# Softmax scaling moved to ScalarE, rotations with one addition, and other slots for the queued stages in a two-layer decoder trunk

## The chip, the cores and the metric

One core of one Trainium2 chip runs the whole program in one launch. The metric is the device time of that launch in microseconds; less is better. The kernel before took 453.48 us, the median of 3 runs.

## What is computed

The reference is a trunk of two layers over 256 positions and 1024 channels, all in float32. Layer 0 projects the input once and feeds two groups of heads: 4 heads of RetNet retention (with a pairwise rotation of queries and keys, a normalisation per head and a SiLU gate) and 8 heads of latent attention (low-rank queries and keys, a rotary part of 64 channels, causal softmax, SiLU gate). Layer 1 is an attention of 16 heads with 64 channels, whose queries and keys are rotated; with 256 positions its block selection comes down to causal softmax over the own block. Each layer ends in a LayerNorm of the scaled input plus the layer's output.

```python
def rope(x, pos):
    ang = pos[:, None, :, None] * inv
    cos, sin = jnp.cos(ang), jnp.sin(ang)
    x1, x2 = x[..., : d // 2], x[..., d // 2:]
    return jnp.concatenate([x1 * cos - x2 * sin, x1 * sin + x2 * cos], -1)
...
s = jnp.where(kpos[None, :] <= qpos[:, None], s, NEG)
p = jax.nn.softmax(s, axis=-1)
return jnp.einsum('bhqk,bhkd->bhqd', p, v)
```

## The kernel before, in words

**Products.** Every product of float32 matrices is three TensorE products: each operand is split into a high part (ScalarE's Copy into a rounded type, L165) and a low part (the rest, by VectorE, L166), and `mm3` (L158 to L162) adds high by high, low by high and high by low into the same PSUM tile. This split is made of every weight tile (names w_h and w_l, from the loaded tile raw) and of every intermediate that is multiplied again.

**Weights.** They come over SyncE's queue in units of mostly 128x1024 numbers, in the order of a list made ahead. A unit is split into one of 6 buffers (WBUFS), so ScalarE's copy of a unit into w_h can start only when TensorE has finished the unit six before it. In the odd layer a unit is 24 products of 256 columns.

**Order of the work.** TensorE's order is the order of the program text. VectorE's and ScalarE's orders come from a scheduler, which places their instructions by its own estimate; each engine then runs its list strictly in order. Work that hangs on earlier results is not written where it arises but handed to a list with `add(task, wait)`: `tick()`, which is called after each unit's products, runs the next piece of the oldest task that is due, and at most one piece that asks for a wait. The constants in L35 to L38 are these waits, counted in ticks: SCO, QR, VAL, LAT1, LAT2, MRG, MPT in the even layer, CROT, CSC, CPT and CAV in the odd one.

**The odd layer.** It runs in 4 quarters q of 4 heads, each of 8 units: two for each of the queries, keys, values (tiles pj) and the gate (pg). `rotated` (L821) applies `rope` (L313) to the projected queries or keys: two multiplications (into crot and rope_b) and two additions of halves into crot (L326). `later` then transposes crot on TensorE (tile pt, 4 transpositions) and splits it to cq_h, cq_l or ck_h, ck_l. `attend_odd` (L781) has three pieces, each for two pairs of heads: `first` writes the scores (tiles sc, 24 small products) and calls `softmax` (L516); `second` transposes the probabilities (`prob_T`, tiles ppt, 12 transpositions, split to pT_h, pT_l); `third` multiplies them with the values (poc), gates (cog, with cgate) and splits the result (oT). CPT[q] ticks stand between the first piece and the second, CAV between the second and the third. PSUM tiles of the tag "at" (sc, ppt, pt, poc and more) share 4 buffers.

**Softmax.** For each pair of heads VectorE takes the masked, negated scores and their minimum (L528), ScalarE the exponential with its sum (L531), VectorE doubles and inverts the sums (L534, L535) and multiplies the probabilities by the inverse (L538): 2 heads x 2 blocks of rows, of 128 and 256 columns, in place. There are 4 such calls in the even layer and 8 in the odd one, so 24 heads and 48 instructions of L538.

**Rotation tables.** At the program's start `angles` (L276) reduces the angles twice, once for 128x64 and once for 128x256 numbers, with 9 VectorE instructions each, and the negated sine is a further VectorE instruction (L306, L311). In the even layer `retention` (L432) rotates its queries and keys with two additions of halves (L451), and `merge` (L487) multiplies the normalised heads (ro) with their gate and transposes them.

Of the kernel before, what the change touches and what calls it, by code (L numbers as in the profile page):

```python
# [9 lines left out]
F32 = mybir.dt.float32  # L10
# [3 lines left out]
AF = mybir.ActivationFunctionType  # L14
OP = mybir.AluOpType
AX = mybir.AxisListType

P = 128
S = 256
NT = S // P  # L20
# [9 lines left out]
MAGIC = 12582912.0  # L30
PI_HI = 3.1415925
WBUFS = 6
TAIL = 5
HOLD = 5
SCO = 7, 4, 4, 5  # L35
CPT = 2, 2, 2, 4
MRG = 1, 1, 1, 5
LAT1, LAT2, QR, VAL, MSC, MPT, MAV, CROT, CSC, CAV = 3, 4, 8, 2, 1, 3, 1, 1, 1, 2  # L38
WARM = 9

OFF = np.cumsum([0, 1024, 1024, 2048, 2048, 256, 256, 64, 1024])
# [102 lines left out]
def trunk(ctx, tc, x, lng, lnb, w, cst, dec, out):  # L144
    nc = tc.nc
# [3 lines left out]
    wk = even.enter_context(tc.tile_pool(name="even", bufs=1))  # L149
# [76 lines left out]
    halfpi = cp.tile([P, 1], F32, name="halfpi")  # L226
# [21 lines left out]
    def cc(name):  # L248
        a, b = CST[name]
        return cs[:, a:b]  # L250
# [4 lines left out]
    posn_i, pos_i = cc("posn").bitcast(I32), cc("pos").bitcast(I32)  # L255
# [6 lines left out]
    for i, (raw, n, ks, cols) in enumerate(first):  # L262
        k = ks[0]
# [7 lines left out]
        for i2 in range(len(cols) // 288):  # L271
            j = max(i2, int(i == 1))
            for t in range(NT):
                mm3(pm[t][j][:, :288], x_rows(k), wv, lambda z: z[:, t * P:(t + 1) * P],
                    lambda z: z[:, i2 * 288:(i2 + 1) * 288], start=k == 0, stop=k == KD - 1)
    def angles(dst_cos, dst_sin, ang, shape):  # L276

        k = wk.tile(shape, F32, name="ang_k", tag="neg", bufs=4)
        nc.vector.tensor_scalar(k, ang, 1.0 / (2 * math.pi), MAGIC, op0=OP.mult, op1=OP.add)
        nc.vector.tensor_scalar(k, k, -MAGIC, None, op0=OP.add)  # L280
        rest = 2 * math.pi
        parts = []
        for bits in (2.0 ** -2, 2.0 ** -5, 2.0 ** -15, 2.0 ** -22):
            c = math.floor(rest / bits) * bits
            parts.append(c)
            rest -= c
        parts.append(rest)
        for c in parts:
            nc.vector.scalar_tensor_tensor(ang, k, -c, ang, op0=OP.mult, op1=OP.add)
        nc.vector.tensor_scalar(ang, ang, -PI_HI, PI_HI, op0=OP.max, op1=OP.min)  # L290
        nc.vector.scalar_tensor_tensor(k, ang, -1.0, ang, op0=OP.mult, op1=OP.max)
        nc.scalar.activation(dst_sin, ang, AF.Sin)
        nc.scalar.activation(dst_cos, k, AF.Sin, bias=halfpi, scale=-1.0)

    H2 = MR // 2
    cosr = wk.tile([P, S], F32, name="cosr")
    sinr = wk.tile([P, 2, S], F32, name="sinr")
    cosn = cp.tile([P, NT, H2], F32, name="cosn")
    sinn = cp.tile([P, NT, 2, H2], F32, name="sinn")
    posn = cp.tile([P, NT], F32, name="posn")  # L300
    nc.vector.tensor_copy(posn, posn_i)
    angn = wk.tile([P, NT, H2], F32, name="angn", tag="neg", bufs=4)
    for t in range(NT):
        nc.vector.tensor_scalar(angn[:, t, :], cc("inv"), posn[:, t:t + 1], None, op0=OP.mult)
    angles(cosn, sinn[:, :, 0, :], angn, [P, NT, H2])
    nc.vector.tensor_scalar(sinn[:, :, 1, :], sinn[:, :, 0, :], -1.0, None, op0=OP.mult)  # L306
    ang = wk.tile([P, S], F32, name="ang", tag="neg", bufs=4)
    nc.vector.tensor_copy(ang, pos_i)
    nc.vector.tensor_scalar(ang, ang, cc("inv_r"), None, op0=OP.mult)
    angles(cosr, sinr[:, 0, :], ang, [P, S])  # L310
    nc.vector.tensor_scalar(sinr[:, 1, :], sinr[:, 0, :], -1.0, None, op0=OP.mult)  # L311

    def rope(src, t, nt, nh, dst, tag=None):  # L313

        b = wk.tile([P, nt * nh * MR], F32, name="rope_b", tag=tag or f"rope_b{nt * nh}")

        def v(z, d):
            return z.rearrange("p (t n d) -> p t n d", t=nt, d=d)

        c4 = cosn[:, t:t + nt, None, :].to_broadcast([P, nt, 2 * nh, H2])  # L320
        nc.vector.tensor_tensor(v(dst, H2), v(src, H2), c4, op=OP.mult)
        s4 = sinn[:, t:t + nt, :, :].rearrange("p t a d -> p t (a d)")[:, :, None, :].to_broadcast([P, nt, nh, MR])
        nc.vector.tensor_tensor(v(b, MR), v(src, MR), s4, op=OP.mult)
        bv, dv = [z.rearrange("p (n a d) -> p n a d", a=2, d=H2) for z in (b, dst)]
        for i in range(2):
            nc.vector.tensor_tensor(dv[:, :, i, :], dv[:, :, i, :], bv[:, :, 1 - i, :], op=OP.add)  # L326

    def transposed(srcs, n, hi, lo):

# [102 lines left out]
    def retention(h, mid=None):  # L432
# [12 lines left out]
        for n, p in enumerate(v4):  # L445
            a = wk.tile([P, 2, S], F32, name="rot_a", tag="rot_a")
            b = wk.tile([P, 2, S], F32, name="rot_b", tag="rot_b")
            nc.vector.tensor_tensor(a, p, cosr[:, None, :].to_broadcast([P, 2, S]), op=OP.mult)
            nc.vector.tensor_tensor(b, p, sinr, op=OP.mult)
            for i in range(2):  # L450
                nc.vector.tensor_tensor(a[:, i, :], a[:, i, :], b[:, 1 - i, :], op=OP.add)  # L451
            qkT.append([z[:, 2 * n:2 * n + 2, :] for z in both])
            split_to(*qkT[n], a)
        qT, kT = qkT
# [61 lines left out]
    def softmax(sc, scale, tag, pb):  # L516
# [18 lines left out]
        nc.vector.reciprocal(rinv, sm)  # L535
        for j in range(nh):
            for i, (a, b) in enumerate(parts):
                nc.vector.tensor_scalar(prob[:, j, a:b], prob[:, j, a:b], rinv[:, i, j:j + 1], None, op0=OP.mult)  # L538
        return prob

    def causal_scores(o, q, k):
# [384 lines left out]
```

## Time and profile before

| | before |
|---|---|
| runs | 453.01, 453.48 and 2466.26 us; median 453.48 |
| the profiled execution | 453.44 us |
| its span (first to last instruction) | 451.7 us |
| granted TensorE clock, mean over the span | 0.994 |
| TensorE busy | 440.0 us |
| VectorE busy | 342.9 us |
| ScalarE busy | 230.0 us |

The 1.74 us between the profiled execution and its span lie outside of the instructions. Times in the rows below are counted from the span's start. Matmuls are pipelined, so one of them shows as longer than the distance to the next one; a wait of TensorE is therefore read from the distance of two starts, compared with the same distance elsewhere.

### The profile page before, as it was taken

Reading aid. Unit: us, or ns where it says so; the run is one execution under the profiler, and the core shown is the slowest. Engines: PE = TensorE matmul, PEld = TensorE weight load, DVE = VectorE, ACT = ScalarE, POOL = GpSimd, SP = SyncE. Lnnn points to the kernel's source line nnn. Section 1 sums busy time; section 2 is a strip of 40 time slices with the busy share of each in tenths; the row PEclk is TensorE's granted clock in tenths of the full one; section 3 lists DMA queues with packets and bytes.
Section 4 is the critical chain, followed back from the end, with each engine's and each line's share of the span. In section 5 each row is a group of like instructions: output and inputs, shape, how many; then the busy total and the mean of one; then the engine's idle time right before and its main releaser. Section 6 shows DMA issues by size and latency. Waiting matters only on the chain.

```text
span 451.7 us, 7705 instructions
## 1 busy us (share of the span) xinstructions
PE 440.0 (97%) x2987; PEld 397.3 (88%) x2987; DVE 342.9 (76%) x663; ACT 230.0 (51%) x386; POOL 10.0 (2%) x18
## 2 busy tenths in 40 slices
PE   8999999999999999999999999999998999999993
PEld 6997889988998888889998888889998999999883
DVE  4899698885878765566697687577997797897847
ACT  5677456553654543435465566214572564744610
POOL 0010000000000000000000000000000000000001
PEclk9999999999999999999999999999998999999999
DMA  8986634544555565555556568705834435354002
GB/s 288 362 226 227 232 131 158 179 121 136 147 181 150 177 229 174 179 186 152 156 156 227 167 202 256 248 1 148 275 123 111 157 125 172 107 187 141 1 0 94
DMA packets 21780, 75.55 MB, mean 167 GB/s; under 512 B 2416, under 2 KB 2800, under 8 KB 21744
## 3 DMA queue, kind: packets, MB, share of 16 engines
q1 hardware_dynamic: 20304, 70.66, 48.7%
q10 hardware_dynamic: 1440, 4.41, 2.9%
q8 instruction: 23, 0.38, 0.3%
q14 instruction: 13, 0.11, 0.1%
HBM read 74.01 MB, written 1.05 MB: 166 GB/s over the span
## 4 chain that ended last, share of the span: by engine, by line
PE 92%; DVE 5%; DMA 1%; ACT 1%; issue 1%; POOL 0%; SPq 0%; DVEq 0%
PE pg L160 5%; PE pg L162 5%; PE pg L161 5%; PE pj L160 5%; PE pj L161 5%; PE pj L162 5%; PE acc L160 4%; PE acc L161 4%; PE acc L162 4%; PE pv L160 3%; PE pv L162 3%; PE pv L161 3%; PE pa L161 2%; PE pa L162 2%; PE pa L160 2%; PE sc L552 2%
## 5 line engine op out<-in xcount | busy, mean ns | idle before, releaser
L166 DVE TENSOR_TENSOR w_l<-raw,w_h 128x1024 fp32r<-128x1024 f32 (+3 forms) x134 | 156.2, 1168 | 59.9 <-ACT w_h L165 59.4
L165 ACT ACTIVATE w_h<-raw 128x1024 fp32r<-128x1024 f32 (+3 forms) x134 | 135.6, 1016 | 115.3 <-issue 32.0
L160 PE MATMUL pj<-w_h,xT_hi 128*128 128x256 f32 x192 | 55.2, 288 | 0.0
L161 PE MATMUL pj<-w_h,xT_lo 128*128 128x256 f32 x192 | 54.0, 281 | 0.0
L162 PE MATMUL pj<-w_l,xT_hi 128*128 128x256 f32 x192 | 53.9, 281 | 0.0
L160 PEld LDWEIGHTS pj<-w_h,xT_hi 128*128 128x128 f32 x192 | 36.7, 191 | 0.2
L161 PEld LDWEIGHTS pj<-w_h,xT_lo 128*128 128x128 f32 x192 | 36.7, 191 | 0.1
L162 PEld LDWEIGHTS pj<-w_l,xT_hi 128*128 128x128 f32 x192 | 36.8, 191 | 0.0
L160 PE MATMUL pv<-w_h,xT_hi 128*128 128x512 f32 x64 | 26.0, 406 | 0.0
L160 PE MATMUL pg<-w_h,xT_hi 128*128 128x512 f32 x64 | 25.8, 403 | 0.0
L162 PE MATMUL pv<-w_l,xT_hi 128*128 128x512 f32 x64 | 25.3, 395 | 0.0
L161 PE MATMUL pv<-w_h,xT_lo 128*128 128x512 f32 x64 | 25.3, 395 | 0.0
L161 PE MATMUL pg<-w_h,xT_lo 128*128 128x512 f32 x64 | 25.3, 395 | 0.0
L162 PE MATMUL pg<-w_l,xT_hi 128*128 128x512 f32 x64 | 25.3, 395 | 0.0
L160 PE MATMUL pg<-xT_hi,w_h 128*128 128x256 f32 x64 | 18.3, 287 | 0.0
L160 PE MATMUL pq<-xT_hi,w_h 128*128 128x256 f32 x64 | 18.2, 284 | 0.0
L160 PE MATMUL pmg<-xT_hi,w_h 128*128 128x256 f32 x64 | 18.1, 283 | 0.0
L161 PE MATMUL pq<-xT_hi,w_l 128*128 128x256 f32 x64 | 17.9, 280 | 0.0
L160 PE MATMUL pkk<-xT_hi,w_h 128*128 128x256 f32 x64 | 17.9, 280 | 0.0
L161 PE MATMUL pkk<-xT_hi,w_l 128*128 128x256 f32 x64 | 17.9, 280 | 0.0
L162 PE MATMUL pmg<-xT_lo,w_h 128*128 128x256 f32 x64 | 17.9, 279 | 0.0
L161 PE MATMUL pmg<-xT_hi,w_l 128*128 128x256 f32 x64 | 17.9, 279 | 0.0
(298 smaller groups left out, 1187.5 us busy)
## 6 DMA issues: line engine op xcount, KB each, us to landing
raw<-w SPq DMA_DIRECT2D x125, 512.0 KB, 3.6
raw<-w SPq DMA_DIRECT2D x7, 416.0 KB, 6.5
raw<-w SPq DMA_DIRECT2D x4, 256.0 KB, 2.7
xn<-x ACTq DMA_DIRECT2D x2, 512.0 KB, 4.3
decay<-dec ACTq DMA_DIRECT2D x1, 512.0 KB, 7.4
decay_ln<-lng ACTq DMA_DIRECT2D x1, 512.0 KB, 6.4
rv_h_ln<-lnb ACTq DMA_DIRECT2D x1, 512.0 KB, 3.9
lng_ln<-lng ACTq DMA_DIRECT2D x1, 512.0 KB, 4.6
```

Source lines behind the costliest of these rows:

```text
L160: nc.tensor.matmul(o, ca(a[0]), cb(b[0]), start=start, stop=False, skip_group_check=True)
L161: nc.tensor.matmul(o, ca(a[1]), cb(b[0]), start=False, stop=False, skip_group_check=True)
L162: state["mm"] = nc.tensor.matmul(o, ca(a[0]), cb(b[1]), start=False, stop=stop, skip_group_check=True)
L165: done = nc.scalar.activation(hi, src, AF.Copy)
L166: nc.vector.tensor_tensor(lo, src, hi.bitcast(F32), op=OP.subtract)
L552: nc.tensor.matmul(o[a][:, c:c + n], q[x][rs, t * P:(t + 1) * P], k[y][rs, :n], start=start and t == 0 and i == 0, stop=i == 2, skip_group ...
```

## The change

It has four parts.

1. `softmax`: the 48 multiplications of the probabilities by the inverse sum go from VectorE (L538) to ScalarE, as a Copy with a scale per row.
2. `rope` and `retention`: the two additions of halves become one addition over the whole tile, which reads the second operand with its halves in reverse. That is 18 additions instead of 36 for the tiles of 128x512, and 2 instead of 4 for the narrow ones of the latent keys.
3. The angles of both rotations lie in one tile of 128x320, reduced once; the negated sines come from ScalarE's Sin with scale -1 instead of from VectorE.
4. The slots: in the odd layer CPT is 3, 4, 4, 4 instead of 2, 2, 2, 4. In the even layer SCO is 6, 4, 4, 6 instead of 7, 4, 4, 5; MRG ends in 6 instead of 5; LAT1 is 5 instead of 3, LAT2 3 instead of 4, QR 10 instead of 8, VAL 3 instead of 2, MPT 2 instead of 3, MAV 2 instead of 1.

```diff
-SCO = 7, 4, 4, 5
-CPT = 2, 2, 2, 4
-MRG = 1, 1, 1, 5
-LAT1, LAT2, QR, VAL, MSC, MPT, MAV, CROT, CSC, CAV = 3, 4, 8, 2, 1, 3, 1, 1, 1, 2
+SCO = 6, 4, 4, 6
+CPT = 3, 4, 4, 4
+MRG = 1, 1, 1, 6
+LAT1, LAT2, QR, VAL, MSC, MPT, MAV, CROT, CSC, CAV = 5, 3, 10, 3, 1, 2, 2, 1, 1, 2
...
+    na = S + NT * H2
+    ang = wk.tile([P, 2 * S], F32, name="ang", tag="rot_a")[:, :na]
+    rounds = wk.tile([P, 2 * S], F32, name="rounds", tag="rot_b")[:, :na]
...
+    for cos, sin, z, za in ((cosn, [sinn[:, :, i, :] for i in range(2)], angn, absn),
+                            (cosr, [sinr[:, i, :] for i in range(2)], ang[:, :S], rounds[:, :S])):
+        for i, d in enumerate(sin):
+            nc.scalar.activation(d, z, AF.Sin, scale=(1.0, -1.0)[i])
+        nc.scalar.activation(cos, za, AF.Sin, bias=halfpi, scale=-1.0)
...
-        for i in range(2):
-            nc.vector.tensor_tensor(dv[:, :, i, :], dv[:, :, i, :], bv[:, :, 1 - i, :], op=OP.add)
+        nc.vector.tensor_tensor(dv, dv, bv[:, :, ::-1, :], op=OP.add)
...
-            for i in range(2):
-                nc.vector.tensor_tensor(a[:, i, :], a[:, i, :], b[:, 1 - i, :], op=OP.add)
+            nc.vector.tensor_tensor(a, a, b[:, ::-1, :], op=OP.add)
...
-                nc.vector.tensor_scalar(prob[:, j, a:b], prob[:, j, a:b], rinv[:, i, j:j + 1], None, op0=OP.mult)
+                nc.scalar.activation(prob[:, j, a:b], prob[:, j, a:b], AF.Copy, scale=rinv[:, i, j:j + 1])
```

On TensorE no instruction is added or removed; 2782 rows stand in another order. In the first quarter of the odd layer 72 products stand between the scores and the transposed probabilities where 48 stood, and the transposed queries follow after 24 more, as before; they now come 48 products after the last product of the queries instead of 24. In the second and third quarter, too, the transposed probabilities come 48 products later, and the transposed keys now have 24 products between them and the scores that read them; before there were 48 in the quarters q = 1, 2 and 3.

**VectorE in the first quarter of the odd layer**, from the rotation of the second quarter's queries on (crot, rope_b) to their low part after the transposition (cq_l); before:

```order
L166 TENSOR_TENSOR w_l<-raw,w_h 128x1024
L321 TENSOR_TENSOR crot<-pj,cosn 128x512
L323 TENSOR_TENSOR rope_b<-pj,sinn 128x512
L166 TENSOR_TENSOR w_l<-raw,w_h 128x1024
L166 TENSOR_TENSOR pT_l<-ppt,pT_h 128x384 x3
L326 TENSOR_TENSOR crot<-crot,rope_b 128x8x32 x2
L166 TENSOR_TENSOR pT_l<-ppt,pT_h 128x384
L166 TENSOR_TENSOR w_l<-raw,w_h 128x1024
L166 TENSOR_TENSOR cq_l<-pt,cq_h 128x512
```

And of the change:

```order
L319 TENSOR_TENSOR crot<-pj,cosn 128x512
L321 TENSOR_TENSOR rope_b<-pj,sinn 128x512
L166 TENSOR_TENSOR w_l<-raw,w_h 128x1024
L323 TENSOR_TENSOR crot<-crot,rope_b 128x512
L166 TENSOR_TENSOR w_l<-raw,w_h 128x1024 x2
L166 TENSOR_TENSOR pT_l<-ppt,pT_h 128x384 x4
```

The addition that completes the queries stands ahead of the low parts of the transposed probabilities (pT_l), where three of these stood ahead of it.

**VectorE at the end of the second quarter**, from the split of the attention's result (oT_l) to the scores' minima (neg); before:

```order
L166 TENSOR_TENSOR oT_l<-cog,oT_h 128x256 x2
L166 TENSOR_TENSOR w_l<-raw,w_h 128x1024
L166 TENSOR_TENSOR ck_l<-pt,ck_h 128x512
L166 TENSOR_TENSOR w_l<-raw,w_h 128x1024
L166 TENSOR_TENSOR cv_l<-pj,cv_h 128x512
L166 TENSOR_TENSOR w_l<-raw,w_h 128x1024
L528 ISA neg,csm_m<-sc,cs 128x128
```

And of the change:

```order
L166 TENSOR_TENSOR oT_l<-cog,oT_h 128x256 x2
L166 TENSOR_TENSOR w_l<-raw,w_h 128x1024
L166 TENSOR_TENSOR cv_l<-pj,cv_h 128x512
L166 TENSOR_TENSOR ck_l<-pt,ck_h 128x512
L166 TENSOR_TENSOR w_l<-raw,w_h 128x1024
L524 ISA neg,csm_m<-sc,cs 128x128
```

One split of weights fewer stands between the keys' low part (ck_l) and the scores, and the values' low part (cv_l) has come ahead of it.

**ScalarE in the last quarter**, from the last exponential (csm) to the split of the attention's result; before:

```order
L531 ACTIVATE prob,csm_s<-neg,csm_m 128x256
L415 ACTIVATE cgate<-pg 128x512
L165 ACTIVATE w_h<-raw 128x1024
L165 ACTIVATE pT_h<-ppt 128x384 x4
L165 ACTIVATE w_h<-raw 128x1024 x2
L165 ACTIVATE oT_h<-cog 128x256 x2
```

And of the change:

```order
L527 ACTIVATE prob,csm_s<-neg,csm_m 128x256
L534 ACTIVATE prob<-prob,csm_i 128x128
L534 ACTIVATE prob<-prob,csm_i 128x256
L534 ACTIVATE prob<-prob,csm_i 128x128
L534 ACTIVATE prob<-prob,csm_i 128x256
L412 ACTIVATE cgate<-pg 128x512
L165 ACTIVATE w_h<-raw 128x1024
L534 ACTIVATE prob<-prob,csm_i 128x128
L534 ACTIVATE prob<-prob,csm_i 128x256
L534 ACTIVATE prob<-prob,csm_i 128x128
L534 ACTIVATE prob<-prob,csm_i 128x256
L165 ACTIVATE pT_h<-ppt 128x384 x4
```

The second pair's four copies stand behind the gate and a split of weights, and ahead of the split of what TensorE transposes from them.

## Rows read from the trace of the kernel before

**Rows 1.** The page's part 1: busy us (share of the span) xinstructions.

```profile
PE 440.0 (97%) x2987; PEld 397.3 (88%) x2987; DVE 342.9 (76%) x663; ACT 230.0 (51%) x386; POOL 10.0 (2%) x18
```

**Rows 2.** Waits of TensorE: us in total, times, longest us.

```profile
PE pt L335 <- DVE crot L326: 2.4, 1, 2.4
```

**Rows 3.** Windows: length, busy PE, PEld, DVE, ACT, POOL, granted clock, DMA.

```profile
340.00:345.00 5.00, 4.22 (x24) 4.25 (x25) 2.93 (x5) 0.60 (x1) 0.00 (x0) 0.66 0.59 179
...
390.00:410.00 20.00, 19.90 (x178) 19.73 (x177) 18.96 (x40) 11.45 (x23) 0.00 (x0) 1.00 0.41 144
...
440.00:451.70 11.70, 4.47 (x34) 4.08 (x33) 8.65 (x19) 0.00 (x0) 1.82 (x2) 0.91 0.25 90
```

**Rows 4.** Timeline of TensorE in the first quarter: start us, duration us, what, idle before.

```profile
338.06 0.28 PE L162 MATMUL pj<-w_l,xT_hi 128*128 128x256 f32 x1
340.78 1.09 PE L335 MATMUL pt<-cs,crot 128*128 128x128 f32 x4 [2.45 <-DVE crot L326]
341.52 0.56 PE L160 MATMUL pj<-w_h,xT_hi 128*128 128x256 f32 x1
...
345.48 0.28 PE L160 MATMUL poc<-pT_h,cv_h 128*64 128x256 f32 x1
```

**Rows 5.** Timeline of VectorE and ScalarE in the first quarter.

```profile
339.89 0.75 DVE L326 TENSOR_TENSOR crot<-crot,rope_b 128x256 f32<-128x256 f32 x2
...
333.55 2.00 ACT L165 ACTIVATE w_h<-raw 128x1024 fp32r<-128x1024 f32 x2
```

**Rows 6.** Timeline of TensorE at the first head's merge.

```profile
62.74 0.28 PE L162 MATMUL pmg<-xT_lo,w_h 128*128 128x256 f32 x1
63.38 1.39 PE L335 MATMUL pt<-cs,ro 128*128 128x128 f32 x8 [0.36 <-DVE ro L491]
64.52 0.36 PE L160 MATMUL pmg<-xT_hi,w_h 128*128 128x256 f32 x1
```

**Rows 7.** Timeline of TensorE in the second quarter, at the transposed keys.

```profile
378.78 0.28 PE L162 MATMUL pj<-w_l,xT_hi 128*128 128x256 f32 x1
379.16 0.63 PE L335 MATMUL pt<-cs,crot 128*128 128x128 f32 x4
```

**Rows 8.** Groups by line and shape: count, busy us, mean ns, idle before.

```profile
L326 DVE TENSOR_TENSOR crot<-crot,rope_b 128x256 f32<-128x256 f32 x16 | 6.0, 416 | 0.0
L538 DVE TENSOR_SCALAR prob<-prob,csm_i 128x256 f32<-128x256 f32 x16 | 5.6, 347 | 0.0
...
L538 DVE TENSOR_SCALAR prob<-prob,csm_i 128x128 f32<-128x128 f32 x16 | 4.5, 284 | 0.3
...
L531 ACT ACTIVATE prob<-neg,csm_m 128x256 f32<-128x256 f32 x16 | 7.9, 496 | 0.0
L531 ACT ACTIVATE prob<-neg,csm_m 128x128 f32<-128x128 f32 x16 | 6.3, 392 | 6.0 <-DVE csm_m L528 6.0
```

**Rows 9.** Timeline of ScalarE: two Copies with a scale per row, then a split.

```profile
34.90 0.82 ACT L372 ACTIVATE lat_h<-pt,cs 128x256 fp32r<-128x256 f32 x2
35.62 1.06 ACT L165 ACTIVATE w_h<-raw 128x1024 fp32r<-128x1024 f32 x1
```

**Rows 10.** Timeline of ScalarE and TensorE in the last quarter.

```profile
420.10 0.58 ACT L415 ACTIVATE cgate<-pg 128x512 f32<-128x512 f32 x1
420.58 1.05 ACT L165 ACTIVATE w_h<-raw 128x1024 fp32r<-128x1024 f32 x1
...
422.55 1.47 PE L559 MATMUL ppt<-cs,prob 128*128 128x128 f32 x12
```

**Rows 11.** Timeline of TensorE and VectorE from the transposed keys to the scores.

```profile
350.50 0.60 PE L335 MATMUL pt<-cs,crot 128*128 128x128 f32 x4
350.86 0.36 PE L160 MATMUL pj<-w_h,xT_hi 128*128 128x256 f32 x1
...
352.99 0.68 DVE L166 TENSOR_TENSOR ck_l<-pt,ck_h 128x512 fp32r<-128x512 f32 x1
...
353.77 0.28 PE L160 MATMUL pg<-xT_hi,w_h 128*128 128x256 f32 x1
```

More of the change, by code (lines that the diff above doesn't have):

```diff
@@ L275, in trunk @@
                     lambda z: z[:, i2 * 288:(i2 + 1) * 288], start=k == 0, stop=k == KD - 1)
[L276 to L293, printed above, removed]
     H2 = MR // 2
@@ L300, in trunk @@
     posn = cp.tile([P, NT], F32, name="posn")
+    na = S + NT * H2
+    ang = wk.tile([P, 2 * S], F32, name="ang", tag="rot_a")[:, :na]
+    rounds = wk.tile([P, 2 * S], F32, name="rounds", tag="rot_b")[:, :na]
     nc.vector.tensor_copy(posn, posn_i)
-    angn = wk.tile([P, NT, H2], F32, name="angn", tag="neg", bufs=4)
     for t in range(NT):
[L304 to L311, printed above, removed]
+        nc.vector.tensor_scalar(ang[:, S + t * H2:S + (t + 1) * H2], cc("inv"), posn[:, t:t + 1], None, op0=OP.mult)
+    nc.vector.tensor_copy(ang[:, :S], pos_i)
+    nc.vector.tensor_scalar(ang[:, :S], ang[:, :S], cc("inv_r"), None, op0=OP.mult)
+    nc.vector.tensor_scalar(rounds, ang, 1.0 / (2 * math.pi), MAGIC, op0=OP.mult, op1=OP.add)
+    nc.vector.tensor_scalar(rounds, rounds, -MAGIC, None, op0=OP.add)
+    rest = 2 * math.pi
+    parts = []
+    for bits in (2.0 ** -2, 2.0 ** -5, 2.0 ** -15, 2.0 ** -22):
+        c = math.floor(rest / bits) * bits
+        parts.append(c)
+        rest -= c
+    parts.append(rest)
+    for c in parts:
+        nc.vector.scalar_tensor_tensor(ang, rounds, -c, ang, op0=OP.mult, op1=OP.add)
+    nc.vector.tensor_scalar(ang, ang, -PI_HI, PI_HI, op0=OP.max, op1=OP.min)
+    nc.vector.scalar_tensor_tensor(rounds, ang, -1.0, ang, op0=OP.mult, op1=OP.max)
+    angn, absn = [z[:, S:].rearrange("p (t d) -> p t d", t=NT) for z in (ang, rounds)]
+    for cos, sin, z, za in ((cosn, [sinn[:, :, i, :] for i in range(2)], angn, absn),
[3 more added lines that the diff above has]
+        nc.scalar.activation(cos, za, AF.Sin, bias=halfpi, scale=-1.0)
     def rope(src, t, nt, nh, dst, tag=None):
```

## The prediction

> **What bounds the kernel now.** I read the page's engine times first. TensorE is busy for 440.0 of 451.7 us, VectorE for 342.9, ScalarE for 230.0 [rows 1]. The change takes no product away, so TensorE's own work is a floor. All that it can win is time in which TensorE stands still or is slow, and the second view, TensorE's waits, says where to look: the largest is one of 2.4 us on the addition that completes a rotated tile, crot [rows 2]. The last 11.7 us, in which TensorE is busy for 4.47 only [rows 3], are the two LayerNorms at the end, which the change leaves alone. So I went through TensorE's timeline for starts that lie further apart than the same starts elsewhere, and found four places.
>
> The first is the big wait. Equal products start 0.12 us apart; here the transposition starts 2.72 us after the product before it, so 2.60 are lost [rows 4]. Behind it the granted clock is 0.66 over five microseconds, against 1.00 in quieter stretches [rows 3], that is, part of it ran at the lower of the two levels, 1.2 GHz, after TensorE had stood still. Its price: the four transpositions take 0.74 us (340.78 to 341.52) where they take 0.36 elsewhere, and the unit of 24 products behind them 3.96 (341.52 to 345.48) where it takes 2.91 [rows 4, 11]. That is 0.38 + 1.05 = 1.43. The place costs 4.03 in all.
>
> The second is at the first head's merge: the transpositions start 0.64 after the last product instead of 0.12, and the eight take 1.14 to the next product [rows 6] where four take 0.36 elsewhere [rows 11], so eight 0.72. Together 0.52 + 0.42 = 0.94. The third and fourth are transposed keys in the second and third quarter, 0.38 instead of 0.12 after the last product (the one in the second quarter) [rows 7]: 0.26 each, 0.52 for both.
>
> The four places hold 4.03 + 0.94 + 0.52 = 5.49 us. That is the most that the change can win.
>
> **The change part by part.**
>
> **Probabilities on ScalarE.** VectorE loses 48 instructions. In the odd layer 16 of 0.347 and 16 of 0.284 [rows 8], 10.1 us; with the even layer's 16 of like length about 15. Four quarters share the 10.1, so each has 2.5 us more room where VectorE was busy for 18.96 of 20 us [rows 3]. TensorE doesn't run on VectorE's share, so the 15 us count nothing by themselves; what counts is what they unblock. ScalarE gains 48 Copies with a scale per row. The nearest row for that is L372: two of 256 columns occupy it for 0.72 us up to the next instruction (34.90 to 35.62), 0.36 each [rows 9]. For 128 columns I take the difference of the two exponentials off, 0.496 - 0.392 = 0.10 [rows 8], and get 0.26; a pair 0.62, four Copies 1.24. Upper end: the exponentials' full durations, 0.89 a pair. Lower end: 0.52 a pair, should Copies of SBUF data overlap better than L372's from PSUM.
>
> Where are they in the way? In the last quarter, whose slot stays. The exponentials end at 420.10 [rows 10]. Now come four Copies (421.34), the gate, whose successor starts 0.48 later (421.82), a split of weights, about 0.95 (422.77), and the second pair's four Copies, the first head's done at 423.4, the second's at 424.0. TensorE starts its 12 transpositions at 422.55 [rows 10], some 0.1 apart, so it wants the second pair's first head at 423.2 and its second head's larger block at 423.65, later by what it waited. I take a wait of 0.5. With the lower price it is 0.1; with the upper one the last Copy ends at 420.10 + 1.78 + 0.48 + 0.95 + 1.78 = 425.1, a wait of 1.45.
>
> In the first quarter the exponentials end at 333.55 and two splits of weights follow, 0.95 apart [rows 5]. With the Copies around the first of them the last Copy ends at 333.55 + 1.24 + 0.95 + 1.24 = 336.98. The transposed probabilities, now one unit later, start at about 337.0 (338.18, when the transposed queries were due, less 1.2 for 12 transpositions; the unit moves from behind them to ahead of them) and want the last block one microsecond later. No wait; with the upper price 0.1.
>
> **One addition per rotation.** Two of 0.416 [rows 8] become one of 512 columns. A forward operation on two tensors of that size takes 0.68 (ck_l) [rows 11]. No row shows a reversed read: 0.68 if it costs nothing, 0.83 if it is as slow as the two, 1.2 if each element took twice as long. I take 0.7. VectorE is not the end of the chain, so 18 times -0.1 is nothing by itself; the cover is gone only where TensorE waits for that addition.
>
> **The slots and the order.** The big wait goes twice over: the transposed queries are due one unit later, at 338.18 + 2.91 = 341.09, and the addition no longer stands behind three low parts of probabilities, where it ended at 340.64 (339.89 + 0.75) [rows 5]. What is late next is the PSUM tile: the transposition needs back the buffer of the first transposed probabilities, which VectorE's first pT_l frees. ScalarE reaches pT_h after two more splits, at 336.98 + 1.9 = 338.9, ends it at 339.4; VectorE has one more w_l of 1.2 ahead of pT_l and frees the buffer at about 340.7, before 341.09. So 2.60 and, as TensorE doesn't stand still, 1.43 are won; with the upper price of the Copies 0.65 come back.
>
> At the first head the retention's products now come one unit earlier (SCO 6, VAL 3 puts po ahead of the last gate unit), so ro and the gate meet well before the merge: 0.94 won. In the second and third quarter the keys' addition is two units old when they are transposed: 0.52 won.
>
> The slots also cost. The keys have 24 products instead of 48 between their transposition and the scores, in three quarters. In the row of before ck_l ends at 353.67, 3.17 after the transposition's start, and one unit behind the transposition TensorE is at 353.77, 3.27 after it [rows 11]. Now cv_l stands ahead of ck_l, 0.60 more: 3.77. The first products of the scores read ck_h alone, some 0.3 us; so TensorE wants ck_l at about 3.57 and waits 0.2. Three times: 0.6. If VectorE came earlier to both it would be 0, if nothing covers it 0.5 each, 1.5.
>
> The other slots of the even layer move pieces that have a unit or more of room on either side; the merged angles take fewer VectorE instructions in a stretch where TensorE doesn't wait. They count 0, and up to 0.4 either way, the 0.36 us of rows 6 being what a missed slot cost there.
>
> **Sum.** -4.03 - 0.94 - 0.52 + 0.5 + 0.6 = -4.39. Against the profiled execution's 453.44 (451.7 of span and 1.74 around it): 449.1. The median of the runs, 453.48, is the same within 0.04. With no new wait 448.0; with all upper ends 453.44 - 5.49 + 1.45 + 1.5 + 0.65 + 0.1 + 0.4 = 452.1.
>
> By the Trainium skill, ScalarE: Activation LUTs, section Rules for kernel authors, an ACTIVATE costs about 0.3 us and 0.83 ns per element. By that a pair of Copies would be an estimated 0.92, and the last Copy of the last quarter would end at 425.2, a wait of 1.6 instead of 0.5: 450.2. This trace speaks against it: two Copies of 256 occupy ScalarE for 0.72 and not 1.0 [rows 9].
>
> **The rivals.**
>
> Dear Copies. The 0.89 a pair holds, so TensorE waits 1.45 in the last quarter and 0.65 in the first, and standing still lowers the clock once more, 1.43 [rows 3, 4]: 453.44 - 5.49 + 0.6 + 1.45 + 0.65 + 1.43 = 452.1. For it: exponentials of the same size last that long [rows 8]. Against it: rows 9, and a wait of 2.45 us stood before the low clock, not one of 1.45. Its wait in the last quarter is the one that the rule of the Trainium skill, ScalarE: Activation LUTs, section Rules for kernel authors, would bring.
>
> The first wait moves and stays. TensorE is released from the addition and then waits as long for the PSUM tile behind pT_l, with the low clock: 453.44 - 0.94 - 0.52 + 0.5 + 0.6 = 453.1, no change. For it: the margin is only 0.4 us of my own working. Against it: it must be missed by 3 us, more than two splits of weights.
>
> Slower: the keys are late. One unit of cover instead of two decides if VectorE is behind at the end of a quarter. Each microsecond that it comes late to the split ahead of cv_l is one that TensorE stands still, three times. From 1.5 us on (5.49 - 0.5 over three quarters is 1.7, and 0.2 of it is in the sum) the change is slower than before; at 2.5 us, with the clock falling each time, it is 3 x (2.5 + 0.2 + 1.43) = 12.4, and 453.44 - 5.49 + 0.5 + 12.4 = 460.9. For it: VectorE was busy for 95% there [rows 3]. Against it: it loses 2.5 us per quarter, and its split waits for ScalarE's w_h, not for its own queue.
>
> **How the numbers follow.** The forecast, 449.1, gets 0.70, its own range 447.9 to 450.5. Dear Copies 0.14, at 452.1; the moved wait 0.09, at 453.1; late keys 0.05; 0.02 for what I don't see. The range for 8 in 10 reaches from 447.9 to 452.6: it holds the forecast and the dear Copies, and leaves out the other two. About 2%, 9.1 us, is what a measurement of this kernel can tell from no change. Faster by more would need 444.4, below the 448.0 that is left when every wait goes: 0.01. Slower by more needs late keys at their worst: 0.03. Within: 0.96.
>
> **What would show it.** Right: no wait of TensorE over 0.6 us between the warm-up and the LayerNorms; granted clock 1.00 from 340 to 345; Copies of the probabilities that follow each other at 0.26 and 0.36; TensorE waiting in the last quarter for ScalarE's L534, about 0.5, and three times about 0.2 on ck_l. Wrong: a wait over 2 us anywhere in the odd layer, or TensorE's waits gone and the time still 453, which would mean that the starts I counted as lost were not.

## The result and the profile after

The changed kernel takes 449.16 us (median; 449.09 to 449.37), the kernel before 453.25 beside it (the median of four, one of them the 2466.26): a ratio of 0.9918, with a 95% interval from 0.9898 to 0.9937. That is 0.8% faster, less than the 2% that the forecast calls a difference. The profiled execution took 449.13 us, 447.3 of them span.

The table cuts the span of each trace at four starts of TensorE: the first product of the even layer's queries (18.8 us in both kernels), the first product of the odd layer, the first product of the last output projection, and the last product of all. All times in us.

| kernel | even layer | four quarters | output projection | after it | median of the runs |
|---|---|---|---|---|---|
| before | 283.61 | 115.93 | 25.83 | 7.47 | 453.25 |
| the change | 282.48 | 112.00 | 26.59 | 7.48 | 449.16 |
| difference | -1.13 | -3.93 | +0.76 | 0 | |
| predicted | -0.94 | -3.95 | +0.5 | 0 | |

The prediction for the quarters is made of the first wait with its low clock (-4.03), the two waits on keys (-0.52) and the three new ones (+0.6). First, the engine times of the change on the page, which answer to [rows 1].

```profile
PE 438.3 (98%) x2987; PEld 395.9 (89%) x2987; DVE 330.1 (74%) x584; ACT 246.8 (55%) x436; POOL 10.5 (2%) x18
```

VectorE lost 12.8 us, and ScalarE gained 16.8. The span follows neither: it is 4.3 to 4.4 us shorter.

The waits of TensorE in the change (us in total, times, longest us), and below them one of its weight loads:

```profile
PE pidle L237 <- DVE idle L234: 1.2, 1, 1.2
PE pt L332 <- DVE pT_l L166: 0.2, 1, 0.2
...
PEld ppt L555 <- ACT prob L534: 0.5, 2, 0.3
```

The 2.4 us on crot [rows 2] are gone. The largest, pidle, is the warm-up at the start. The timeline of TensorE at the place of the old wait (start us, duration us, what, idle before):

```profile
339.61 0.28 PE L162 MATMUL pj<-w_l,xT_hi 128*128 128x256 f32 x1
340.11 0.66 PE L332 MATMUL pt<-cs,crot 128*128 128x128 f32 x4 [0.22 <-DVE pT_l L166]
340.52 0.37 PE L160 MATMUL pj<-w_h,xT_hi 128*128 128x256 f32 x1
...
343.34 0.28 PE L160 MATMUL poc<-pT_h,cv_h 128*64 128x256 f32 x1
```

The transposed queries start 0.50 us after the last product, where it was 2.72 [rows 4]. Equal products follow at 0.12, so 0.38 us are still lost. The releaser is no longer the addition but pT_l, which frees the PSUM tile. The four transpositions take 0.41 instead of 0.74, and the unit behind takes 2.82 (340.52 to 343.34) instead of 3.96. The windows (length, busy PE, PEld, DVE, ACT, POOL, granted clock, DMA) say why the unit is shorter, against [rows 3]:

```profile
340.00:345.00 5.00, 4.89 (x47) 4.89 (x48) 5.00 (x10) 2.46 (x3) 0.00 (x0) 1.00 0.66 220
390.00:410.00 20.00, 20.00 (x188) 19.82 (x188) 17.34 (x27) 11.72 (x19) 0.00 (x0) 1.00 0.54 172
```

The granted clock is 1.00 instead of 0.66, that is, the engine stays on the higher of its two levels. VectorE is down from 18.96 to 17.34 of 20 us. What led up to the transposition, on ScalarE and on VectorE:

```profile
332.43 1.49 ACT L534 ACTIVATE prob<-prob,csm_i 128x128 f32<-128x128 f32 x4
333.81 1.05 ACT L165 ACTIVATE w_h<-raw 128x1024 fp32r<-128x1024 f32 x1
334.76 1.48 ACT L534 ACTIVATE prob<-prob,csm_i 128x128 f32<-128x128 f32 x4
336.15 1.99 ACT L165 ACTIVATE w_h<-raw 128x1024 fp32r<-128x1024 f32 x2
338.05 1.59 ACT L165 ACTIVATE pT_h<-ppt 128x384 fp32r<-128x384 f32 x4
...
336.04 0.68 DVE L323 TENSOR_TENSOR crot<-crot,rope_b 128x512 f32<-128x512 f32 x1
337.23 2.36 DVE L166 TENSOR_TENSOR w_l<-raw,w_h 128x1024 fp32r<-128x1024 f32 x2 [0.51 <-ACT w_h L165]
339.50 1.95 DVE L166 TENSOR_TENSOR pT_l<-ppt,pT_h 128x384 fp32r<-128x384 f32 x4
```

This is the order that the prediction described: the addition is done at 336.72, more than three microseconds early, and the first pT_l (1.95 / 4, about 0.5) ends at about 340.0, when the transposition starts. The four Copies of a pair of heads take 1.38 us up to the next instruction (332.43 to 333.81).

In the last quarter (ScalarE, then TensorE; the last line is from the kernel before and follows its transpositions), against [rows 10]:

```profile
416.77 1.05 ACT L165 ACTIVATE w_h<-raw 128x1024 fp32r<-128x1024 f32 x1
417.72 1.48 ACT L534 ACTIVATE prob<-prob,csm_i 128x128 f32<-128x128 f32 x4
419.10 1.22 ACT L165 ACTIVATE pT_h<-ppt 128x384 fp32r<-128x384 f32 x3
...
417.48 2.21 PE L555 MATMUL ppt<-cs,prob 128*128 128x128 f32 x12
419.45 0.48 PE L160 MATMUL acc<-w_h,oT_h 128*128 128x512 f32 x1
...
423.78 0.48 PE L160 MATMUL acc<-w_h,oT_h 128*128 128x512 f32 x1
```

The 12 transpositions take 1.97 us (417.48 to 419.45), before 1.23 (422.55 to 423.78): they run behind the second pair's Copies, which start 0.24 later than they. That is 0.74 of the 0.76 us by which the output projection's stretch got longer.

The merge of the first head, against [rows 6], and the keys of the second quarter, against [rows 7], with ck_l and the products of the scores behind them:

```profile
62.58 0.28 PE L162 MATMUL pmg<-xT_lo,w_h 128*128 128x256 f32 x1
62.70 1.03 PE L332 MATMUL pt<-cs,ro 128*128 128x128 f32 x8
63.49 0.36 PE L160 MATMUL pmg<-xT_hi,w_h 128*128 128x256 f32 x1
...
376.68 0.28 PE L162 MATMUL pj<-w_l,xT_hi 128*128 128x256 f32 x1
376.80 0.27 PE L332 MATMUL pt<-cs,crot 128*128 128x128 f32 x1
...
379.76 0.68 DVE L166 TENSOR_TENSOR ck_l<-pt,ck_h 128x512 fp32r<-128x512 f32 x1
...
380.32 0.28 PE L548 MATMUL sc<-ck_h,cq_l 64*128 64x128 f32 x2
380.50 0.33 PE L548 MATMUL sc<-ck_l,cq_h 64*128 64x128 f32 x2
```

The merge starts 0.12 after its product instead of 0.64, and its eight transpositions take 0.79 instead of 1.14: 0.87 won. The keys start at 0.12 too. ck_l ends at 380.44, and the first product that reads it starts at 380.50, 0.18 after the one ahead of it where 0.11 is usual. So the margin that was cut is used up: the 24 products of the scores take 1.64, 1.70 and 1.70 us in the three quarters instead of 1.57, together 0.32 longer.

Groups of the change by line and shape (count, busy us, mean ns), against [rows 8]:

```profile
L534 ACT ACTIVATE prob<-prob,csm_i 128x256 f32<-128x256 f32 x16 | 8.0, 497 | 0.0
...
L534 ACT ACTIVATE prob<-prob,csm_i 128x128 f32<-128x128 f32 x16 | 6.2, 389 | 0.0
...
L323 DVE TENSOR_TENSOR crot<-crot,rope_b 128x512 f32<-128x512 f32 x8 | 5.5, 687 | 0.0
```

### The profile page after: what moved, and what is told of

It is laid out like the page before. It is cut to its first block, busy times and chain, and to the rows that moved or that the text cites. A ratio compares the mean times of both kernels' runs of the same rounds, so it can differ in the third digit from the quotient of the medians.

```text
span 447.3 us, 7696 instructions
## 1 busy us (share of the span) xinstructions
PE 438.3 (98%) x2987; PEld 395.9 (89%) x2987; DVE 330.1 (74%) x584; ACT 246.8 (55%) x436; POOL 10.5 (2%) x18
## 4 chain that ended last, share of the span: by engine, by line
PE 89%; ACT 5%; DVE 3%; issue 2%; DMA 1%; SPq 0%; DVEq 0%; ACTq 0%
PE pg L160 5%; PE pg L162 5%; PE pg L161 5%; PE pj L160 4%; PE pj L161 4%; PE pj L162 4%; PE pv L160 3%; PE acc L160 3%; PE pv L162 3%; PE acc L161 3%; PE pv L161 3%; PE acc L162 3%; PE pa L161 3%; PE pa L162 2%; PE pa L160 2%; PE pt L332 2%
## 5 line engine op out<-in xcount | busy, mean ns | idle before, releaser
L160 PE MATMUL pj<-w_h,xT_hi 128*128 128x256 f32 x192 | 54.3, 283 | 0.0
L162 PE MATMUL pg<-xT_lo,w_h 128*128 128x256 f32 x64 | 17.9, 279 | 0.0
```

Of the source, the lines that this page charges most:

```text
L160: nc.tensor.matmul(o, ca(a[0]), cb(b[0]), start=start, stop=False, skip_group_check=True)
L162: state["mm"] = nc.tensor.matmul(o, ca(a[0]), cb(b[1]), start=False, stop=stop, skip_group_check=True)
```

## The experiments

The theory: the gain is the odd layer's first wait with what hangs on it, and it is the later slots that win it; the Copies on ScalarE win TensorE nothing and cost what they delay. The main rival: the lighter VectorE is what wins, and the slots only go with it. Four kernels ran in each of three groups; the kernel before, beside them, took 453.18, 453.6 and 452.44 us. The table gives their stretches, cut as above. A stretch is that of the one profiled execution, the median is that of all runs; where the two do not go together, the text says so.

| kernel | even layer | four quarters | output projection | median |
|---|---|---|---|---|
| slots alone | 283.43 | 111.69 | 25.84 | 449.21 |
| Copies alone | 284.31 | 122.82 | 26.71 | 461.37 |
| change without Copies | 282.49 | 112.04 | 25.84 | 448.66 |
| the same, second time | 282.49 | 111.77 | 25.84 | 448.54 |
| change, first slot 2 | 282.08 | 113.91 | 26.56 | 451.49 |
| change, last slot 5 | 282.46 | 111.99 | 29.51 | 450.89 |
| odd slots alone | 284.43 | 111.72 | 25.84 | 450.06 |
| change, slots 3, 2, 2, 4 | 282.47 | 116.40 | 26.71 | 454.11 |
| single additions alone | 284.28 | 113.84 | 25.84 | 453.38 |
| the change again | 282.48 | 111.98 | 26.59 | 449.19 |
| no Copies, slots 3, 2, 2, 4 | 282.48 | 111.81 | 25.84 | 448.34 |
| change, even slots of before | 283.33 | 112.12 | 26.58 | 450.21 |

### The slots alone

The new constants in the kernel before, and nothing else.

```diff
-SCO = 7, 4, 4, 5
-CPT = 2, 2, 2, 4
+SCO = 6, 4, 4, 6
+CPT = 3, 4, 4, 4
...
```

> The kernel before with the new slots alone: probabilities stay on VectorE, two additions per rotation, two reductions of angles. Theory (the slots remove TensorE's waits, and the copies on ScalarE only add waits): the first quarter's 4.0 us, the merge's 0.9 and the two waits on the keys, 0.5, go; 0.3 to 0.6 come back at the scores; no wait for probabilities in the last quarter. 448.3 to 448.9 us, below the change's 449.16. Rival (VectorE's relief is what does it): without it VectorE is late for the keys in each quarter, waits of 0.5 us and more there, 450.5 us or more.

Measured: 449.21 us, ratio 0.9919, interval 0.9893 to 0.9945; just above the expected range and far from the rival. The slots alone bring all that the change brings. In the even layer the merge no longer waits, but TensorE waits once for the retention's rotation:

```profile
PE pg L160 <- DVE rot_b L449: 0.4, 1, 0.4
```

This wait does not come from the slots: kernels that keep the even layer's slots of before have it too (the even layer's slots taken back, below).

### The Copies alone

```diff
-                nc.vector.tensor_scalar(prob[:, j, a:b], prob[:, j, a:b], rinv[:, i, j:j + 1], None, op0=OP.mult)
+                nc.scalar.activation(prob[:, j, a:b], prob[:, j, a:b], AF.Copy, scale=rinv[:, i, j:j + 1])
```

> The kernel before with the probabilities normalised on ScalarE alone; slots, rotations and angles as before. Theory: the addition that completes the queries comes earlier on VectorE, so the wait of 2.45 us on it goes, but in the first quarter the transposed probabilities are due at 334.0, and the second pair's copies end only at about 337.3: a new wait of 2.3 to 2.7 us, with or without a low clock behind it (1.4), and 0.7 in the last quarter. 452.0 to 453.7 us. Rival (VectorE's relief is what does it): 449.3 to 450.5 us.

Measured: 461.37 us, ratio 1.0185, interval 1.0148 to 1.0222. That is 7.7 us above the end of the expected range. The waits of TensorE in this kernel, its transposed probabilities in the second and the third quarter, and the windows behind the first and the third:

```profile
PE ppt L559 <- ACT prob L538: 3.4, 3, 1.3
PE pt L335 <- DVE crot L326: 1.4, 2, 0.7
...
364.54 0.98 PE L559 MATMUL ppt<-cs,prob 128*128 128x128 f32 x6
366.80 1.42 PE L559 MATMUL ppt<-cs,prob 128*128 128x128 f32 x5 [1.28 <-ACT prob L538]
...
395.93 0.98 PE L559 MATMUL ppt<-cs,prob 128*128 128x128 f32 x6
398.19 1.53 PE L559 MATMUL ppt<-cs,prob 128*128 128x128 f32 x6 [1.27 <-ACT prob L538]
...
338.00:342.00 4.00, 3.94 (x21) 3.65 (x21) 3.56 (x8) 2.90 (x7) 0.00 (x0) 0.57 0.45 140
399.70:403.20 3.50, 3.50 (x19) 3.50 (x18) 3.00 (x5) 1.97 (x5) 0.00 (x0) 0.51 0.61 177
```

I had looked for the wait in the first and the last quarter only. With two ticks the second pair's Copies come too late in all of the first three: on ScalarE they stand behind a split of weights, which stands behind the first pair's Copies. In each, the second half of the 12 transpositions starts about 2.3 us after the first (364.54 to 366.80) where a run of six takes some 0.6. The granted clock falls behind the first (0.57 over four microseconds) and the third (0.51 over 3.5, the lower level), but not behind the second. The second line of the waits is the transposed keys of the second and third quarter, 0.7 us each. The mechanism had been the expected one, its places had not. So the Copies are no neutral part of the change: without later slots they cost 8.2 us (461.37 - 453.18), twice what the slots win.

### The change without the Copies

The change with L534 on VectorE, as it was; run twice, the second time on one chip with the change itself.

> The change with the probabilities back on VectorE; slots, rotations and angles as in the change. Theory: the wait of 0.74 us in the last quarter and the 0.38 at the transposed queries of the first go, nothing comes back but at the scores: 448.0 to 448.7 us, and 0.5 to 1.1 less than the change. Rival (VectorE's relief is what does it): 450.5 us or more.

Measured: 448.66 us, ratio 0.9907, interval 0.9881 to 0.9932. That is inside the expected range. Whether the 0.5 us to the change's 449.16 come from the kernel, the second run decides, with both on one chip.

> The change itself once more, unaltered, as the neighbour on the same chip for the three kernels beside it: 449.2 us, range 448.8 to 449.8.

> The change with the probabilities scaled on VectorE as before, a second time and beside the change on one chip. Theory (the Copies on ScalarE cost the wait of 0.74 us in the last quarter and win nothing for TensorE elsewhere): 0.3 to 0.8 us below the change measured beside it, about 448.7 us. Rival (the 0.5 us between the two earlier medians were two chips): within 0.2 us of it.

Measured: the change 449.19 (449.0 to 449.53), without the Copies 448.54 (448.02 to 448.87), 0.65 less and without overlap. The output projection's stretch is 25.84 again, that of the kernel before. So the move to ScalarE costs this kernel 0.65 us, and the output projection's stretch (26.59 against 25.84) accounts for it.

### The first slot back at two ticks

```diff
-CPT = 3, 4, 4, 4
+CPT = 2, 4, 4, 4
```

> The change with the first quarter's slot CPT back at 2, all else as in the change. Theory: the 12 transpositions are due one unit of 2.8 us earlier and wait for ScalarE's copies for 2.3 to 2.7 us, the 0.38 at the transposed queries goes, and the clock may fall (1.4): 451.1 to 452.9 us. Rival (the new order on VectorE alone removed the wait, the slot of the first quarter is of no matter): 448.8 to 449.4 us.

Measured: 451.49 us, ratio 0.9972, interval 0.995 to 0.9993. That is inside the expected range. The quarters are 1.91 longer than in the change. Here is the place, where the second half starts 2.34 us after the first instead of 0.6:

```profile
333.33 1.53 PE L555 MATMUL ppt<-cs,prob 128*128 128x128 f32 x6
335.67 1.02 PE L555 MATMUL ppt<-cs,prob 128*128 128x128 f32 x4 [0.80 <-ACT prob L534]
```

No wait on crot comes back: in the change the later first slot is room for the Copies. But TensorE also comes to the queries 2.4 us later here, because it waited for the Copies, so that this run does not show whether the lighter VectorE alone would have been in time. With the probabilities on VectorE it is the later slots that take the wait on crot away (the odd layer's slots alone, below).

### A fifth tick in the last quarter

```diff
-CPT = 3, 4, 4, 4
+CPT = 3, 4, 4, 5
```

> The change with one tick more in the last quarter (CPT 3, 4, 4, 5), nothing else. Theory (the 0.74 us that the last quarter's 12 transpositions lose are a wait for ScalarE's Copies, and 24 products more hide it): those transpositions take 1.23 us again and the time falls by 0.5 to 0.8, to 448.3 to 448.7 us. Rival (the last quarter has no room behind, so that the pieces that follow meet the end of the products and the wait only moves there): 449.1 us or more.

Measured: 450.89 us, ratio 0.9956, interval 0.9937 to 0.9974: 1.7 slower than the change. The Copies' wait is gone and another has taken its place, as the rival had it, though not at the place it named:

```profile
418.98 1.15 PE L555 MATMUL ppt<-cs,prob 128*128 128x128 f32 x9
422.01 0.55 PE L555 MATMUL ppt<-cs,prob 128*128 128x128 f32 x3 [1.88 <-DVE pT_l L166]
```

One unit later, the second half of the output projection has begun, and its last 256 columns take one of the four PSUM tiles of the tag "at". Three are left for four heads, so the fourth head's transpositions wait until VectorE's first pT_l gives a tile back. In the profiled execution the granted clock fell behind this wait, which is in the 29.51 of the table:

```profile
422.70:426.30 3.60, 3.60 (x15) 3.10 (x14) 1.28 (x3) 1.44 (x2) 0.00 (x0) 0.53 0.02 5
```

That execution took 452.13 us; four of the nine runs took 452.13 to 452.46, the other five 450.21 to 450.89, and the median is one of these.

### The odd layer's slots alone

```diff
-CPT = 2, 2, 2, 4
+CPT = 3, 4, 4, 4
```

> The kernel before with CPT 3, 4, 4, 4 alone: the even layer's slots, the Copies on VectorE and the two additions stay as before. Theory (the gain is the odd layer's first quarter, and it hangs on CPT alone; in the run of the slots alone the even layer ended no earlier than before, 302.81 against 302.43 us): 302.43 plus the 145.0 us that the rest took in that run, plus 1.75 around the span, 449.2 us, range 448.7 to 449.8, no low clock in the odd layer. Rival (the even layer's slots carry a microsecond or more of the gain of the slots): 450.2 us or more.

Measured: 450.06 us (449.22 to 451.36), ratio 0.9925, interval 0.9897 to 0.9953. The median lies between the two expectations; the stretches decide. The quarters take 111.72, like those of all slots together (111.69), and four less than before. The transposed queries start 0.17 us after the product ahead of them, where it was 2.72:

```profile
340.83 0.28 PE L162 MATMUL pj<-w_l,xT_hi 128*128 128x256 f32 x1
341.00 0.66 PE L335 MATMUL pt<-cs,crot 128*128 128x128 f32 x4
```

So this one line wins the whole gain of the odd layer, with the probabilities on VectorE and two additions per rotation.

### Two ticks in the second and third quarter, with and without the Copies

```diff
-CPT = 3, 4, 4, 4
+CPT = 3, 2, 2, 4
```

> The change with the two ticks of before in the second and third quarter (CPT 3, 2, 2, 4). Theory (the Copies on ScalarE need the later slots: with 48 products between scores and transposed probabilities TensorE waits about 2.0 us for them in each of the two quarters, as it did with the Copies alone, and the clock falls behind at least one, 1.4 us): 449.2 + 4.0 + 1.4 - 0.3 for the scores that get their second unit back = 454.3 us, range 452.4 to 455.8, with waits of TensorE for L534 in both quarters. Rival (the waits of the run with the Copies alone came from VectorE's fuller list, and with the single additions two ticks are enough): 448.8 to 449.6 us.

> The probabilities on VectorE and CPT 3, 2, 2, 4: the later slot in the first quarter alone. Theory (the slots of 4 in the second and third quarter serve only the Copies, which without them cost 4 to 5 us; without the Copies two ticks hide the softmax): 448.8 us, range 448.4 to 449.5, made of 0.26 won at two scores and 0.38 lost at two keys' transpositions that follow their rotation after 24 products. Rival (VectorE's scaling needs the later slots too): 450.5 us or more, with waits for L534 in these quarters.

Measured: with the Copies 454.11 us (ratio 1.0024, interval 1.0005 to 1.0043), all of the gain lost. The time is the expected one, its parts are not quite: the quarters are 4.4 us longer than in the change, where the theory had 3.7, and the profiled execution (453.23 us) shows none of the low clock that it had for 1.4. Without the Copies 448.34 (0.9905, 0.988 to 0.993), a little under the expected range. It is the lowest median of all kernels here, below both the change and the kernel before; from the 448.54 with the later slots it can't be told apart. The transposed probabilities of the third quarter, with the Copies, then without:

```profile
389.27 0.98 PE L555 MATMUL ppt<-cs,prob 128*128 128x128 f32 x6
391.52 1.53 PE L555 MATMUL ppt<-cs,prob 128*128 128x128 f32 x6 [1.28 <-ACT prob L534]
```

```profile
387.81 1.47 PE L555 MATMUL ppt<-cs,prob 128*128 128x128 f32 x12
389.04 0.36 PE L160 MATMUL pj<-w_h,xT_hi 128*128 128x256 f32 x1
```

Four ticks in these quarters do nothing but hide ScalarE's Copies. Where VectorE scales, two are enough.

### The single additions alone

```diff
-        for i in range(2):
-            nc.vector.tensor_tensor(dv[:, :, i, :], dv[:, :, i, :], bv[:, :, 1 - i, :], op=OP.add)
+        nc.vector.tensor_tensor(dv, dv, bv[:, :, ::-1, :], op=OP.add)
```

and the same in the retention.

> The kernel before with the single additions alone (half 512 columns, second operand read in reverse, 20 instead of 40 instructions). Theory (VectorE's time counts nothing by itself, only the addition that TensorE waits for in the first quarter gets shorter, by about 0.1 us): 453.0 us, range 452.4 to 453.4, with the wait on crot of 2 us and more and the low clock behind it still there, and about 0.69 us per addition. Rival (VectorE bounds the odd layer, so that 18 times 0.145 us come off): 450.6 us.

Measured: 453.38 us, ratio 0.999, interval 0.9974 to 1.0006. No change, as expected of an engine that TensorE mostly doesn't wait for. Its trace has something else: the old wait, and no low clock behind it. The profiled execution took 452.03 us and is one of three of the ten runs with a mean clock of 0.995 or more; the other seven have 0.991 or 0.992 and took 453.29 to 454.14. So the 113.84 of the table is shorter than the 115.93 of before mainly by the clock.

```profile
338.73 0.28 PE L162 MATMUL pj<-w_l,xT_hi 128*128 128x256 f32 x1
341.38 0.63 PE L334 MATMUL pt<-cs,crot 128*128 128x128 f32 x4 [2.38 <-DVE crot L325]
...
340.00:345.00 5.00, 3.62 (x33) 3.65 (x34) 3.65 (x7) 0.91 (x3) 0.00 (x0) 1.00 0.51 145
```

### The even layer's slots taken back

```diff
-SCO = 6, 4, 4, 6
+SCO = 7, 4, 4, 5
...
-LAT1, LAT2, QR, VAL, MSC, MPT, MAV, CROT, CSC, CAV = 5, 3, 10, 3, 1, 2, 2, 1, 1, 2
+LAT1, LAT2, QR, VAL, MSC, MPT, MAV, CROT, CSC, CAV = 3, 4, 8, 2, 1, 3, 1, 1, 1, 2
```

> The change with the even layer's slots of before (SCO, MRG, LAT1, LAT2, QR, VAL, MPT, MAV), CPT 3, 4, 4, 4 kept. Theory (the 0.9 us at the first head's merge are the even slots', together with the lighter VectorE): the odd layer's first product comes at 302.2 to 302.6 us instead of 301.3, and the time is 450.1 us, range 449.8 to 450.6, with the late merge of 0.5 us back. Rival (the single additions and merged angles bring the merge in time by themselves): 449.0 to 449.4 us.

Measured: 450.21 us, ratio 0.9949, interval 0.9931 to 0.9966; 1.02 above the change beside it, and the merge waits again:

```profile
PE pt L332 <- DVE ro L487: 0.4, 1, 0.4
```

The even layer takes 283.33 with the lighter VectorE alone and 282.48 with the slots as well: that is the merge. With the slots alone it takes 283.43, because of the wait on rot_b. That wait is in four traces, all with the old angles (the slots alone, the Copies alone, the single additions alone and the odd slots alone), and in none of the nine that have the merged angles and single additions. The single additions alone did not remove it (0.6 us); the merged angles were not run alone. Nor is it there in each execution: the odd slots alone have the even layer of before, with every instruction of VectorE and ScalarE in the same order, and it took 284.43 against 283.61:

```profile
PE pg L160 <- DVE rot_b L449: 0.8, 1, 0.8
```

So one and the same even layer differs by 0.8 us between two executions, and of the 1.13 by which the change's is shorter only the merge's 0.87 is shown to be won each time.

## Why the prediction was right

The time was predicted at 449.1 and measured at 449.16. The sum stood on the right places and mechanisms; that it fits this closely is luck. The first quarter won 0.34 less than predicted and the Copies cost 0.24 more, while the scores cost 0.28 less and the even layer won 0.19 more. Step by step:

- **The first quarter.** Predicted -4.03, measured -3.69 (2.22 at the wait, 0.33 in the four transpositions, 1.14 in the unit behind). Wait and low clock went, by the order of instructions that the prediction read. The next thing late was the PSUM tile, as it said; but the margin, 0.4 by the prediction, was gone, and 0.38 us of wait stayed, inside the 0.65 that it kept as the upper end. The cause is the Copies: in the change without them, on the same slots, the queries' transposition enters at the usual 0.12.
- **The merge.** Predicted -0.94, measured -0.87; the rest of the even layer's 1.13 was counted as zero. The prediction gave it to the slots, and the runs agree: the wait is gone with the slots alone and back when they are taken back. It put 0.72 for eight transpositions without a wait, where the trace has 0.79. What else the even layer won is within the 0.8 us by which one even layer differs between executions.
- **Keys.** -0.52 as predicted.
- **Copies in the last quarter.** Predicted +0.5, measured +0.74. The place and the mechanism were right; the term was too small because a pair of Copies was taken at 0.62 and takes 0.69 (half of 1.38). The second pair's Copies start 0.24 us after the transpositions, nearly as predicted (0.22).
- **Scores.** Predicted three waits of 0.2 on ck_l, measured 0.07, 0.12 and 0.12.
- **The reversed addition.** Taken as 0.7, measured 0.687, against 0.68 for a forward one of that size.

The Trainium skill's rule of about 0.3 us and 0.83 ns per element (ScalarE: Activation LUTs, section Rules for kernel authors) would have made a pair 0.92; measured are 0.69. The Trainium skill, ScalarE: Activation LUTs, section What ACT_TABLE_LOAD costs, is closer: 186 ns and 0.833 ns per column, 93 more for a scale by pointer, and an overlap of 93 when two follow each other. By this section of the Trainium skill the durations are an estimated 386 and 492 ns, where the trace has 389 and 497, and four in a row 1.38 us, which is what they took.

What the prediction did not see, though its total does not show it, is what the later slots are for. It costed the Copies in the first and the last quarter and called the moved slots of the second and third a price (the scores). What those slots do is hide the Copies, which would otherwise cost TensorE about 4.4 us in the quarters (116.40 against 112.00). It priced the move at 0.5 us in the last quarter and counted VectorE's 2.5 us of room per quarter as nothing by itself; the runs agree, and put the whole move at 0.65 us of loss with nothing on the other side.

Of the rivals, dear Copies had the right sign and a part of the size; the moved wait happened for 0.38 of its 2.6 us; late keys did not happen.

## What to carry to other kernels

Where one engine is busy for 97% of the span, time is won only at its few long gaps: look for the piece of work that is queued one slot too early behind a slow chain, and move it by one slot before making any instruction cheaper. Moving work to an idle engine is not free if it lengthens a chain between two products; test each part alone, since here the visible win and a hidden loss came in one change. And a later slot has its own price: count the buffers that are held at the new place.

## What was not expected of the hardware

**The clock does not fall every time.** In the profiled execution of before the low clock followed the wait of 2.45 us; in that of the single additions a wait of 2.38 at the same place had none. In all the traces together TensorE lost 2.1 to 2.6 us at one place nine times. The granted clock fell behind four of them (before; the Copies alone in the first and third quarter; the fifth tick) and stayed at 1.00 behind five (the single additions; the Copies alone in the second quarter; the first slot at two ticks; the Copies with slots 3, 2, 2, 4, twice). Which of them it will be is not shown. Of the 54 runs of the kernel before that stand beside the experiments, 32 have a mean granted clock of 0.990 to 0.992 and a median of 453.71 us, and 22 have 0.994 to 0.996 and 452.06. The 1.65 between them is near the 1.43 that the prediction read from the rows. Of the ten runs of the change none is below 0.994. Those other runs have no trace, so that the same stretch is meant is inferred; but the runs of the fifth tick, which fall into two groups in the same way, support it, as their profiled execution with the low stretch is in the slower one. The mean alone does not sort every run, since the profiled one of before, low stretch and all, has 0.994. It also counts the low clock after the last product, and that is longer in some executions than in others: from 440 us on the granted clock is 0.91 before [rows 3] and 0.65 in the change. By these two groups the change wins about 2.9 us where the clock held (452.06 - 449.16) and 4.5 where it fell (453.71 - 449.16); the prediction took a price that is paid in some runs for one that is always paid. The Trainium skill, TensorE: Matmul & The Clock Gate, section What's actually happening, says that the activity which the gate watches is not counted from the kernel's start, so that one kernel comes out differently from run to run. The two groups agree with it; no run here shows how the gate counts.

**A second operand read with its halves in reverse costs nothing that shows**: 687 ns for 128x512 numbers and 688 in the retention, against 0.68 us for a forward operation of that size.
